# Seven raw input blocks in a state space layer, later list transposes and joined last value blocks: one decoder step on one core

## The chip, the cores and the metric

One core of a Trainium2 chip runs one launch of the kernel. The metric is the time on the device in microseconds (us). The kernel before was timed three times: 2629.93, 2630.28 and 2636.83, median 2630.28.

## The reference

One inference step of a two-layer trunk for 304 tokens: 16 meta tokens, 8 samples of 4 tokens, a prompt of 256. All numbers are float32, the width is 1024.

- Layer 0: rms norm, RWKV-7 time mixing, added to h; then rms norm and a PEER feed-forward, added to h.
- Layer 1: the same with a Mamba-2 state space layer (`in_proj` to 5152 columns, a causal convolution of width 4 with Silu on 3072 of them, decays from `softplus(dt)`, a chunked scan over 32 heads in 4 groups, a gate `silu(z)`, a group norm, `out_proj`), then PEER again and a final rms norm.

```python
def rms_norm(x, g):
    y = x * rsqrt(mean(x * x, -1) + 1e-5)
    return y * g
# state space layer
zxbcdt = xn @ in_proj
conv = conv_b + sum(full[:, j:j + L] * conv_w[j] for j in range(4))
xbc = silu(conv); dt = softplus(dt_raw + dt_bias)
# PEER: 8 heads, two lists of 128 keys per head, the 16 best sums of 16 x 16 pairs
sv, si = top_k(s, 16); cand = sv[:, :, 0, :, None] + sv[:, :, 1, None, :]
top_s, pos = top_k(cand, 16); gate = softmax(top_s)
out = sum over the 128 chosen experts e of  gate_e * gelu(x . u_e) * v_e
```

An rms norm is one divisor per token, so that `(h*g/rms) @ w` is `((h*g) @ w)/rms`: a product can be made from `h*g` and divided afterwards.

## The kernel before

Rows live with features on partitions and tokens along the free axis. Products that need float32 are made of three passes: weight and row are split in a high part (`whi`, `xh`, a cast on ACT at L279) and the rest (`wlo`, `xl`, a subtraction on DVE at L286 or on POOL at L284); `mm3` (L301) issues 24 matmuls for a block of 128 output columns, first 16 with `whi`, then 8 with `wlo`. Raw weights come by SP's DMA queue into three buffers (`wraw`); `whi` and `wlo` have two each.

**PEER (`peer`, run once per layer).** Its instructions are ordered by a planner that plays them on a timeline (L1687); what `keep_in_program_order` marks stays where the text has it. After the norm and the queries come 56 blocks `s_chunk(b)` of expert scores: 24 matmuls into `psc` (L305, L306, L308), Gelu on ACT (L1080), and `wlo` wholly on POOL. Beside them DVE runs three list searches as generators (`topk(0)` for 48 or fewer single tokens, `topk(1)` and `topk(2)` for 128 prompt tokens each), one or two steps a block. Each ends with three late pieces (L1018 to L1048): `exps` on ACT (an exponential with its table load), `gates` on DVE (sum, reciprocal, product, L1022 to L1024) and for lists 1 and 2 `finish`: three transposes on PE (`ptk`, L1029) of the row index `af`, the column index `bf` and the gate `ts`, and a copy into `sel` (L1032). The table `AFTER` at L1090 says behind which block each list's three pieces stand: list 1 at 29, 31, 39, list 2 at 46, 46, 52. After block 55 come the one-hot products (`onehots`, L1104, `pwt` at L1135), which read `sel`, and then 128 value blocks.

**The end of PEER.** The value blocks (L1248 to L1289) add 12 matmuls each into four accumulators `acc[i]` (token half `i // 2`, column half `i % 2`), in the order of the three passes; only block 127 is sorted by `i`. After it, layer 0 copies the accumulators (ACT and DVE in turn), transposes them (`pot`, L1314) and adds them to h (L1317); layer 1 adds them to rows (L1299) and norms these (`normed`, L1210).

**The state space layer (`mamba`).** It has no planner of its own; the scheduler orders each engine by readiness and by the order of the text. `prenorm` (L333) makes `xh`, `xl` from `h*g`, before the rms is known; the squares, the first product and the rms follow (`rmsnorm`, L310). `proj(blk)` makes one block of `in_proj`. The first `NU = 4` blocks (40, 32, 36, 16) use the rows that are not yet divided; their readers multiply by `ri`, the reciprocal of the rms (L1386, L1417). When the fifth begins (L1363), `xh` and `xl` are split anew from `xn = h*g*ri`, which `rmsnorm` has made (L331), with a high priority. Raw weights 40 and 32 are split at the very start, their `wlo` on POOL (L284). `decays` (L1409) makes from block 40 a long chain of small DVE instructions: the softplus as a polynomial (L1424 to L1434), two scans, and `L` and `R` (L1447 to L1452); then for each of 4 groups, 3 chunks and 2 halves a masked copy `rh` of `R` on POOL (L1489), a product `pe` on PE (L1492, L1493) and an exponential into `E` on ACT (L1494). `conv` (L1376) reads a block, convolves it on DVE (L1394) and applies Silu on ACT (L1397 three times 32 columns, L1400, L1401).

Of the kernel before, what the change touches and what calls it, by code (L numbers as in the profile page):

```python
# [23 lines left out]
F32 = mybir.dt.float32  # L24
F32R = mybir.dt.float32r
# [3 lines left out]
AF = mybir.ActivationFunctionType  # L29
ALU = mybir.AluOpType  # L30
# [4 lines left out]
T = 304  # L35
TP = 320
D = 1024
KB = 8
# [28 lines left out]
def chain(*gens):  # L67
    for g in gens:
        yield from g
# [157 lines left out]
class K:  # L227
# [102 lines left out]
        for k in range(KB) if out is not None else ():  # L330
            nc.vector.scalar_tensor_tensor(out[:, k], h[:, k], self.vec(g, k), ri, op0=ALU.mult, op1=ALU.mult)  # L331

    def prenorm(self, out, h, g, xh, xl, sq, rr, tag, mid):  # L333

        nc = self.nc
        for k in range(KB):
            x = nc.scalar.activation(xh[:, k], h[:, k], AF.Copy, scale=self.vec(g, k))
            self.tc.keep_in_program_order(x)
            nc.vector.scalar_tensor_tensor(xl[:, k], h[:, k], self.vec(g, k), xh[:, k].bitcast(F32), op0=ALU.mult, op1=ALU.subtract)
        self.rmsnorm(out, h, g, sq, None, tag, rr, mid)  # L340
        return rr[1]

# [508 lines left out]
    def peer(self, l, ng):  # L851

        nc, tc, a, C, V = self.nc, self.tc, self.a, self.C, self.nc.vector
# [233 lines left out]

        tk = chain(topk(0), topk(1), topk(2))

        AFTER = ((14, 16, 55), (29, 31, 39), (46, 46, 52))  # L1090
        for b in range(B0):
            s_chunk(b, G[:, b], leng=LP if b < LB else None, tag="so"[b % 2])
            next(tk, None)
# [142 lines left out]
        def slot():  # L1236
# [5 lines left out]
            used[r] = now[1]  # L1242
            return 4 * r

        ggen = chain(gather_u(range(ng)), gather())
        nleft = 128 - B0 - NF
        done = 0
        for b in range(128):  # L1248
            while done < nleft and (done <= (b + 1) * nleft // 118 or B0 + NF + done <= b + 1):
                t = hs[:, done % 2 * 256:done % 2 * 256 + 256]  # L1250
                s_chunk(B0 + NF + done, t, leng=LS, tag="sm"[done % 2])
                V.tensor_mul(G[:, B0 + NF + done], G[:, B0 + NF + done], t)
                done += 1
            if b == 112 and last:
                gfin = gview(24, (128, D))
                nc.sync.dma_start(gfin, a["nfin"].to_broadcast([128, D]))
            if b == (120 if last else 122):
                nc.sync.dma_start(self.h, hd)
            if b == 124 and last:

                ht = []
                for i in range(2):
                    t = gview(32 + 4 * i, (128, D))
                    for half in range(2):
                        ph = self.bank([128, 512], "ph", "s")
                        for k in range(4):
                            mm(ph[:, k * 128:k * 128 + 128], lhsT=self.h[:, 4 * half + k, 48 + 128 * i:176 + 128 * i], rhs=C["eye"],  # L1267
                               is_transpose=True, start=True, stop=True)
                        nc.scalar.copy(t[:, half * 512:half * 512 + 512], ph)
                    ht.append(t)  # L1270

                nc.scalar.activation(fin[:, 3, 3:4], C["cst"][:, 0:1], AF.Sqrt)
            raw = self.wp.tile([128, 8, 128], F32, name="wraw", tag="wraw", bufs=3) if b < RB else gview(32 + 4 * (b % RN), (128, 8, 128))
            nc.sync.dma_start(raw, a[f"v{l}"][b].rearrange("a (k d) -> a k d", d=128))
            vh = self.wp.tile([128, 8, 128], F32R, name="whi", tag="whi")
            vl = self.wp.tile([128, 8, 128], F32R, name="wlo", tag="wlo")
            self.split(vh, vl, raw, leng=LV)
            gh = tp.tile([128, 256], F32R, name="gh", tag="w1", bufs=W1)
            gl = tp.tile([128, 256], F32R, name="glo", tag="w2", bufs=W1)
            self.split(gh, gl, G[:, b])  # L1280

            vhf, vlf = (w.rearrange("p k d -> p (k d)") for w in (vh, vl))
            todo = [(i, g, w) for g, w in ((gh, vhf), (gl, vhf), (gh, vlf)) for i in range(4)]
            if b == 127:
                todo.sort(key=lambda x: x[0])
            for i, g, w in todo:
                t0, d0 = i // 2 * 128, i % 2 * 512
                mm(acc[i], lhsT=g[:, t0:t0 + 128], rhs=w[:, d0:d0 + 512], start=b == 0 and g is gh and w is vhf,  # L1288
                   stop=b == 127 and w is vlf)  # L1289
            now[0] = b  # L1290
            while b >= G0 and stepped <= (b - G0) * steps // (G1 - G0):
                next(ggen, None)
                stepped += 1
# [9 lines left out]
        for i, pt in enumerate(self.gpt):  # L1303
            hk = self.h[:, 4 * i:4 * i + 4, 0:16 * ng].rearrange("p k (g t) -> p k g t", t=16)
            V.tensor_add(hk, hk, pt.rearrange("p k (g t) -> p k g t", t=32)[:, :, 0:ng, 0:16])
        for i in range(4):
            ot = gview(100 + 2 * i, (128, 512))
            if i % 2:
                V.tensor_copy(ot, acc[i])
            else:  # L1310
                nc.scalar.copy(ot, acc[i])
            pt = self.bank([128, 4, 128], "pot", "s")
            for j in range(4):
                mm(pt[:, j], lhsT=ot[:, j * 128:(j + 1) * 128], rhs=C["eye"], is_transpose=True, start=True, stop=True)  # L1314
            t0 = 48 + i // 2 * 128
            hk = self.h[:, i % 2 * 4:i % 2 * 4 + 4, t0:t0 + 128]
            V.tensor_add(hk, hk, pt)  # L1317
# [3 lines left out]
    def mamba(self):  # L1321
# [15 lines left out]
        tok = pp.tile([128, 3, 128], F32, name="tok")  # L1337
        cdb = pp.tile([128, 10, 32], F32, name="cdb")
        mk = pp.tile([128, 3, 128], BF, name="mk")
        V.tensor_copy(mk[:, 2], C["eye"])  # L1340
        self.psum(i=2, G=2, f=2, t=2)
        ep = st.enter_context(tc.tile_pool(name="ep", bufs=4, reuse_waits="tile"))

# [2 lines left out]
        TM = T - M0  # L1346
        LM = 8
        LE = 8
        NU = 4
        done = [0]  # L1350
        pre = {b: self.load_w(a["win"][b], leng=LE, raw=raws[b]) for b in (40, 32)}
        xn = ep.tile([128, KB, T], F32, name="xn", tag="E")
        rr = ep.tile([128, 2, T], F32, name="rr", tag="E")

        def proj(blk):

            if done[0] and blk == 40:
                return first.pop()
            w = pre.pop(blk) if blk in pre else self.load_w(a["win"][blk], leng=LE if done[0] < LM else None,
                                                                    raw=raws.get(blk))  # L1360
            c0 = M0 if blk < 16 else 0
            p = self.bank([128, T - c0], "pi", "i" if done[0] % NU < 2 or done[0] >= NU else "f")
            if done[0] == NU:  # L1363
                with tc.high_priority(offset=200):
                    for k in range(KB):
                        self.split(xh[:, k], xl[:, k], xn[:, k])
            done[0] += 1
            self.mm3(p, w, (xh[:, :, c0:], xl[:, :, c0:]))
            return p

        first = []
        ri = self.prenorm(xn, self.h, "nm1", xh, xl, ep.tile([128, KB, T], F32, name="sq", tag="E"), (rr[:, 0], rr[:, 1]), "t",
                          lambda: first.append(proj(40)))
        gp = st.enter_context(tc.tile_pool(name="mg", bufs=2, reuse_waits="tile"))

        def conv(blk):  # L1376
# [16 lines left out]
            for j in range(1, 4):  # L1393
                V.scalar_tensor_tensor(ac, s[:, j:j + 328], self.vec("cw", 24 * j + blk), ac, op0=ALU.mult, op1=ALU.add)  # L1394
            r = gp.tile([128, 384], F32, name="xc", tag="xc", bufs=8)
            for c in range(3):
                nc.scalar.activation(r[:, 32 * c:32 * c + 32].rearrange("p (b t) -> p b t", t=4),  # L1397
                                     ac[:, 0:56].rearrange("p (b t) -> p b t", t=7)[:, :, 0:4], AF.Silu)

            nc.scalar.activation(r[:, 96:128], ac[:, 56:88], AF.Silu)  # L1400
            nc.scalar.activation(r[:, 128:384], ac[:, 72:328], AF.Silu)  # L1401
# [5 lines left out]
        E = []  # L1407

        def decays(dp):  # L1409
# [6 lines left out]
            x = t384("x"); xs = t384("xs")[:, 0:T]  # L1416
            V.tensor_mul(xs, p, ri)  # L1417
            tc.keep_in_program_order(V.tensor_copy(mk[:, 0:2], nm))
            p = xs
            for dst, src in ((x[:, 0:96].rearrange("p (c t) -> p c t", t=32), p[:, None, 16:48].to_broadcast([128, 3, 32])),  # L1420
                             (x[:, 96:128], p[:, 0:32]), (x[:, 128:384], p[:, 48:T])):
# [60 lines left out]
            for g in range(4):  # L1482
                Eg = ep.tile([128, 3, 8, 128], F32, name="E", tag="E")
                for ti in range(3):
                    ts = slice(ti * 128, ti * 128 + 128)
                    for q in range(2):
                        h4 = slice(8 * g + 4 * q, 8 * g + 4 * q + 4)
                        rh = dp.tile([128, 4, 128], F32, name="rh", tag="rh", bufs=2)
                        P.tensor_mul(rh, R[:, None, ts].to_broadcast([128, 4, 128]),  # L1489
                                     C["dl"][:, h4][:, :, None].to_broadcast([128, 4, 128]))  # L1490
                        pe = self.bank([128, 4, 128], "pe", "G")
                        mm(pe, lhsT=L[:, ts], rhs=rh, start=True, stop=False)  # L1492
                        mm(pe, lhsT=mk[:, 2], rhs=mk[:, min(ti, 1)][:, None, :].to_broadcast([128, 4, 128]), start=False, stop=True)  # L1493
                        nc.scalar.activation(Eg[:, ti, 4 * q:4 * q + 4], pe, AF.Exp)  # L1494
                E.append(Eg)
# [224 lines left out]
```

## Time and profile before

| | |
|---|---|
| median of the three runs | 2630.28 us |
| the profiled execution | 2634.19 us |
| its span, first to last instruction | 2632.3 us |
| mean granted TensorE clock, as a share of full speed | 0.974 |
| PE busy | 2477.9 us (94%) |
| DVE busy | 1898.8 us (72%) |
| ACT busy | 1253.6 us (48%) |
| POOL busy | 1008.2 us (38%) |

Times in the rows below are us from the first instruction. Busy means that an engine has an instruction under way; matmuls are pipelined, so that a busy PE can still run at half its clock. A wait is the idle time of an engine just before an instruction, put down to the engine and line that released it. The layers lie at: RWKV to 413, PEER of layer 0 from 413 to 1331, the state space layer to 1700, PEER of layer 1 to the end.

### The profile page before, as it was taken

Reading aid. Unit: us, or ns where it says so; the run is one execution under the profiler, and the core shown is the slowest. Engines: PE = TensorE matmul, PEld = TensorE weight load, DVE = VectorE, ACT = ScalarE, POOL = GpSimd, SP = SyncE. Lnnn points to the kernel's source line nnn. Section 1 sums busy time; section 2 is a strip of 40 time slices with the busy share of each in tenths; the row PEclk is TensorE's granted clock in tenths of the full one; section 3 lists DMA queues with packets and bytes.
Section 4 is the critical chain, followed back from the end, with each engine's and each line's share of the span. In section 5 each row is a group of like instructions: output and inputs, shape, how many; then the busy total and the mean of one; then the engine's idle time right before and its main releaser. Section 6 shows DMA issues by size and latency. Waiting matters only on the chain. (4 is left out here: it accounts for less than half of the span.)

```text
span 2632.3 us, 47459 instructions
## 1 busy us (share of the span) xinstructions
PE 2477.9 (94%) x18281; PEld 2137.4 (81%) x18281; DVE 1898.8 (72%) x3724; ACT 1253.6 (48%) x2384; POOL 1008.2 (38%) x863
## 2 busy tenths in 40 slices
PE   7999999996989999999978988999889899999998
PEld 4677768996978888888864886989789788888886
DVE  5355556797695678788784887769949756776777
ACT  3322223453784444444456543335448644444444
POOL 4111110495980233533146555117769401223210
PEclk9999999998999999999989999999989999999999
DMA  3111115453416788888732443555543267787774
GB/s 142 51 45 50 47 55 170 141 183 121 134 40 215 250 312 309 299 306 299 273 110 80 156 164 118 160 177 154 168 122 98 84 213 257 255 285 268 261 265 157
DMA packets 125858, 460.34 MB, mean 175 GB/s; under 512 B 14816, under 2 KB 15744, under 8 KB 122432
## 3 DMA queue, kind: packets, MB, share of 16 engines
q1 hardware_dynamic: 99488, 360.75, 42.1%
q0 software_dynamic: 26144, 96.56, 10.2%
q8 instruction: 144, 2.36, 0.4%
q14 instruction: 82, 0.67, 0.1%
HBM read 440.70 MB, written 16.56 MB: 174 GB/s over the span
## 5 line engine op out<-in xcount | busy, mean ns | idle before, releaser
L279 ACT CAST whi<-wraw 128x1024 fp32r<-128x1024 f32 (+1 forms) x619 | 642.1, 1038 | 870.7 <-PE acc L1288 312.9
L286 DVE TENSOR_TENSOR wlo<-wraw,whi 128x1024 fp32r<-128x1024 f32 (+1 forms) x493 | 593.7, 1204 | 397.2 <-ACT whi L279 339.6
L305 PE MATMUL psc<-xh,whi 128*128 128x256 f32 x2048 | 506.6, 285 | 3.1 <-ACT h L1080 2.6
L306 PE MATMUL psc<-xl,whi 128*128 128x256 f32 x2048 | 504.8, 283 | 0.0
L284 POOL TENSOR_TENSOR wlo<-wraw,whi 128x1024 fp32r<-128x1024 f32 (+1 forms) x150 | 355.1, 2374 | 176.5 <-ACT whi L279 91.0
L305 PEld LDWEIGHTS psc<-xh,whi 128*128 128x128 f32 x2048 | 388.0, 189 | 10.0 <-ACT h L1080 3.1
L306 PEld LDWEIGHTS psc<-xl,whi 128*128 128x128 f32 x2048 | 388.6, 190 | 5.5
L1066 POOL DMA_INDIRECT G<-in_un,gi x80 | 114.5, 1432 | 468.5 <-DVE glo L286 304.6
L1288 PE MATMUL acc<-whi,glo 128*128 128x512 f32 x1024 | 285.1, 399 | 6.7 <-DVE glo L286 6.7
L308 PE MATMUL psc<-xh,wlo 128*128 128x256 f32 x2048 | 290.3, 283 | 0.0
L1288 PE MATMUL acc<-whi,gh 128*128 128x512 f32 x1024 | 283.9, 398 | 1.9 <-ACT gh L279 1.0
L1288 PE MATMUL acc<-wlo,gh 128*128 128x512 f32 x1024 | 281.8, 397 | 0.0
L308 PEld LDWEIGHTS psc<-xh,wlo 128*128 128x128 f32 x2048 | 263.0, 188 | 0.5 <-issue 0.3
L1288 PEld LDWEIGHTS acc<-whi,glo 128*128 128x128 f32 x1024 | 193.8, 190 | 54.8 <-DVE glo L286 7.6
L1288 PEld LDWEIGHTS acc<-wlo,gh 128*128 128x128 f32 x1024 | 192.7, 189 | 47.8 <-DVE wlo L286 1.3
L1163 POOL DMA_INDIRECT G<-in_v,gi x80 | 117.0, 1463 | 298.2 <-DVE G L1158 163.8
L1288 PEld LDWEIGHTS acc<-whi,gh 128*128 128x128 f32 x1024 | 185.0, 189 | 40.3 <-ACT whi L279 1.6
L1135 PE MATMUL pwt<-ob,oa 128*128 128x128 f32 x1024 | 144.8, 282 | 11.6 <-DVE ob L1109 7.8
L1135 PEld LDWEIGHTS pwt<-ob,oa 128*128 128x128 f32 x1024 | 127.8, 191 | 23.2 <-issue 19.3
L305 PE MATMUL pi<-xh,whi 128*128 128x304 f32 (+1 forms) x328 | 102.5, 331 | 11.7 <-ACT xh L279 3.7
L286 DVE TENSOR_TENSOR glo<-G,gh 128x256 fp32r<-128x256 f32 x256 | 106.9, 419 | 2.7 <-ACT gh L279 2.7
L279 ACT CAST gh<-G 128x256 fp32r<-128x256 f32 x256 | 101.8, 399 | 11.7 <-PE acc L1288 11.6
(484 smaller groups left out, 4444.0 us busy)
## 6 DMA issues: line engine op xcount, KB each, us to landing
wraw<-in_u SPq DMA_DIRECT2D x256, 512.0 KB
wraw<-in_v SPq DMA_DIRECT2D x256, 512.0 KB
wraw<-in_win SPq DMA_DIRECT2D x41, 512.0 KB
wraw<-in_wq SPq DMA_DIRECT2D x32, 512.0 KB
wraw<-in_rkv SPq DMA_DIRECT2D x24, 512.0 KB
h<-in_ssm SPq DMA_DIRECT2D x8, 1024.0 KB
out_sssm<-h POOLq DMA_DIRECT2D x8, 1024.0 KB
wraw<-in_wo SPq DMA_DIRECT2D x8, 512.0 KB
```

Source lines behind the costliest of these rows:

```text
L279: self.nc.scalar.copy(hi, x)
L284: self.nc.gpsimd.tensor_sub(lo[:, :n], x[:, :n], hi[:, :n].bitcast(F32))
L286: self.nc.vector.tensor_sub(lo[:, n:], x[:, n:], hi[:, n:].bitcast(F32))
L305: nc.tensor.matmul(ps, lhsT=whi[:, k], rhs=xhi[:, x0 + k], start=start and k == 0, stop=False)
L306: nc.tensor.matmul(ps, lhsT=whi[:, k], rhs=xlo[:, x0 + k], start=False, stop=False)
L308: nc.tensor.matmul(ps, lhsT=wlo[:, k], rhs=xhi[:, x0 + k], start=False, stop=stop and k == kb - 1)
L1066: nc.gpsimd.indirect_dma_start(out=rows, out_offset=None, in_=a[f"un{l}"], in_offset=bass.IndirectOffsetOnAxis(ap=gi[:, 0, g, m:m + 1], ax ...
L1135: mm(pw[:, j], lhsT=oa[:, j], rhs=ob[:, j], start=True, stop=True)
L1163: nc.gpsimd.indirect_dma_start(out=rows, out_offset=None, in_=vrows, in_offset=bass.IndirectOffsetOnAxis(ap=gi[:, 1, g, m:m + 1], axis=0))
L1288: mm(acc[i], lhsT=g[:, t0:t0 + 128], rhs=w[:, d0:d0 + 512], start=b == 0 and g is gh and w is vhf, stop=b == 127 and w is vlf)
```

## The change

The list transposes move (`AFTER`), the last two value blocks are joined and sorted by accumulator, seven blocks instead of four use the undivided rows, the second split is made piece by piece behind them without a priority, the two first `wlo` go from POOL to DVE behind `xl`, the cast of the unit matrix `mk[:, 2]` moves behind the mask's, three Silu become one that reads a repeated operand, and every third `rh` is made by four ACT instructions instead of one of POOL.

```diff
-    def prenorm(self, out, h, g, xh, xl, sq, rr, tag, mid):
+    def prenorm(self, out, h, g, xh, xl, sq, rr, tag, mid, then=None):
...
             nc.vector.scalar_tensor_tensor(xl[:, k], h[:, k], self.vec(g, k), xh[:, k].bitcast(F32), op0=ALU.mult, op1=ALU.subtract)
+        if then is not None:
+            then()
         self.rmsnorm(out, h, g, sq, None, tag, rr, mid)
...
-        AFTER = ((14, 16, 55), (29, 31, 39), (46, 46, 52))
+        AFTER = ((14, 16, 55), (29, 31, 52), (45, 45, 55))
...
+        ORD = (0, 1, 2, 3) if last else (0, 2, 1, 3)
...
-            if b == 127:
-                todo.sort(key=lambda x: x[0])
+
+            if b == 126:
+                kept = todo
+                todo = []
+            elif b == 127:
+                todo = sorted(kept + todo, key=lambda x: ORD.index(x[0]))
...
-        for i in range(4):
+        for n, i in enumerate(ORD):
             ot = gview(100 + 2 * i, (128, 512))
-            if i % 2:
+            if n % 2:
...
-        V.tensor_copy(mk[:, 2], C["eye"])
...
-        NU = 4
+        NU = 7
         done = [0]
-        pre = {b: self.load_w(a["win"][b], leng=LE, raw=raws[b]) for b in (40, 32)}
-        xn = ep.tile([128, KB, T], F32, name="xn", tag="E")
+        pre = {}
+        for b in (40, 32):
+            pre[b] = tuple(self.wp.tile([128, KB, 128], F32R, name=n, tag=n) for n in ("whi", "wlo"))
+            nc.scalar.copy(pre[b][0], raws[b])
+
+        def lows():
+            for b in (40, 32):
+                tc.keep_in_program_order(V.tensor_sub(pre[b][1], raws[b], pre[b][0].bitcast(F32)))
...
-            p = self.bank([128, T - c0], "pi", "i" if done[0] % NU < 2 or done[0] >= NU else "f")
+            p = self.bank([128, T - c0], "pi", "i" if done[0] % 4 < 2 or done[0] >= NU else "f")
             if done[0] == NU:
-                with tc.high_priority(offset=200):
-                    for k in range(KB):
-                        self.split(xh[:, k], xl[:, k], xn[:, k])
+                for k in range(KB):
+                    xn = gp.tile([128, T], F32, name="xn", tag="xdt", bufs=3)
+                    V.scalar_tensor_tensor(xn, self.h[:, k], self.vec("nm1", k), ri, op0=ALU.mult, op1=ALU.mult)
+                    self.split(xh[:, k:k + 1], xl[:, k:k + 1], xn[:, None])
...
-        ri = self.prenorm(xn, self.h, "nm1", xh, xl, ep.tile([128, KB, T], F32, name="sq", tag="E"), (rr[:, 0], rr[:, 1]), "t",
-                          lambda: first.append(proj(40)))
+        ri = self.prenorm(None, self.h, "nm1", xh, xl, ep.tile([128, KB, T], F32, name="sq", tag="E"), (rr[:, 0], rr[:, 1]), "t",
+                          lambda: first.append(proj(40)), lows)
...
-            for c in range(3):
-                nc.scalar.activation(r[:, 32 * c:32 * c + 32].rearrange("p (b t) -> p b t", t=4),
-                                     ac[:, 0:56].rearrange("p (b t) -> p b t", t=7)[:, :, 0:4], AF.Silu)
+            nc.scalar.activation(r[:, 0:96].rearrange("p (c b t) -> p c b t", b=8, t=4),
+                                 ac[:, 0:56].rearrange("p (b t) -> p b t", t=7)[:, None, :, 0:4].to_broadcast([128, 3, 8, 4]), AF.Silu)
...
             tc.keep_in_program_order(V.tensor_copy(mk[:, 0:2], nm))
+            V.tensor_copy(mk[:, 2], C["eye"])
...
-                        P.tensor_mul(rh, R[:, None, ts].to_broadcast([128, 4, 128]),
-                                     C["dl"][:, h4][:, :, None].to_broadcast([128, 4, 128]))
+                        if (6 * g + 2 * ti + q) % 3 == 0:
+                            for j in range(4):
+                                nc.scalar.activation(rh[:, j], R[:, ts], AF.Copy, scale=C["dl"][:, h4.start + j:h4.start + j + 1])
+                        else:
+                            P.tensor_mul(rh, R[:, None, ts].to_broadcast([128, 4, 128]),
+                                         C["dl"][:, h4][:, :, None].to_broadcast([128, 4, 128]))
```

## Rows read from the trace of the kernel before

**Rows 1.** Who PE waited for, over the whole span: waiting line, the releaser, us in total, times, the longest.

```profile
PE ptk L1029 <- DVE G L1024: 20.5, 2, 10.2
PE ptk L1029 <- DVE G L1016: 19.3, 2, 9.8
...
PE pe L1492 <- POOL rh L1489: 7.0, 3, 2.8
...
PE pi L306 <- DVE xl L339: 3.8, 1, 3.8
PE pi L305 <- ACT xh L279: 3.7, 1, 3.7
...
PE px L1637 <- ACT xc L1400: 3.4, 1, 3.4
...
PE ptk L1029 <- DVE G L1017: 3.0, 1, 3.0
```

**Rows 2.** PE in order of time around the list transposes, layer 0, the first one-hot products of layer 0, and layer 1: start, us, engine, line, operation, tiles, shapes, count, idle time before and its releaser.

```profile
607.37 0.27 PE L1029 MATMUL ptk<-c,G 128*128 128x128 f32 x1
...
628.15 0.47 PE L1029 MATMUL ptk<-c,G 128*128 128x128 f32 x1 [10.24 <-DVE G L1024]
...
669.26 0.39 PE L1135 MATMUL pwt<-ob,oa 128*128 128x128 f32 x2
...
1897.95 0.33 PE L1029 MATMUL ptk<-c,G 128*128 128x128 f32 x1 [3.01 <-DVE G L1017]
...
1918.49 0.48 PE L1029 MATMUL ptk<-c,G 128*128 128x128 f32 x1 [10.23 <-DVE G L1024]
```

**Rows 3.** Stretches of the span: its length, then us busy (and instructions) of PE, PEld, DVE, ACT and POOL, then the granted PE clock, the DMA share and GB/s.

```profile
500.00:600.00 100.00, 100.00 (x844) 100.00 (x843) 100.00 (x405) 52.32 (x76) 88.89 (x36) 1.00 0.61 185
607.00:628.00 21.00, 1.11 (x7) 0.59 (x5) 20.96 (x42) 0.99 (x2) 2.68 (x2) 0.60 0.19 61
628.00:640.00 12.00, 11.85 (x86) 11.86 (x87) 10.62 (x11) 7.22 (x16) 7.68 (x6) 0.84 0.19 53
...
1918.50:1930.00 11.50, 11.50 (x84) 11.50 (x85) 10.42 (x10) 7.22 (x16) 7.65 (x6) 0.84 0.18 46
...
1357.00:1389.00 32.00, 22.21 (x122) 20.57 (x122) 31.85 (x55) 20.39 (x57) 17.37 (x30) 0.86 0.16 50
1389.00:1436.00 47.00, 40.24 (x122) 18.75 (x122) 16.23 (x20) 29.77 (x49) 34.67 (x32) 0.89 0.14 45
```

**Rows 4.** DVE in order of time, layer 0: three pairs of the same line and shape, the first of each pair made while POOL was at work, or L1024 the other way round (the columns of rows 2).

```profile
585.97 3.43 DVE L1007 TENSOR_TENSOR G<-G 128x1920 bf16<-128x1920 bf16 x1
...
608.31 3.96 DVE L1011 TENSOR_TENSOR G<-G,cp 128x2048 bf16<-128x2048 f32 x1
...
620.49 1.22 DVE L1007 TENSOR_TENSOR G<-G 128x1920 bf16<-128x1920 bf16 x1
...
625.60 2.29 DVE L1011 TENSOR_TENSOR G<-G,cp 128x2048 bf16<-128x2048 f32 x1
627.80 0.29 DVE L1024 TENSOR_TENSOR G<-G 128x128 f32<-128x128 f32 x1
...
655.39 0.29 DVE L1022 TENSOR_REDUCE G<-G 128x8 f32<-128x128 f32 x1 [16.74 <-ACT G L1019]
...
655.95 1.57 DVE L1024 TENSOR_TENSOR G<-G 128x128 f32<-128x128 f32 x1
```

**Rows 5.** Groups of instructions over the whole span: line, engine, operation, tiles, shapes, count, then us busy, the mean ns of one, and the idle time of the engine before them.

```profile
L286 DVE TENSOR_TENSOR wlo<-wraw,whi 128x1024 fp32r<-128x1024 f32 (+1 forms) x493 | 593.7, 1204 | 397.2 <-ACT whi L279 339.6 <-PE psc L308 35.9 <-issue 5.0
...
L284 POOL TENSOR_TENSOR wlo<-wraw,whi 128x1024 fp32r<-128x1024 f32 (+1 forms) x150 | 355.1, 2374 | 176.5 <-ACT whi L279 91.0 <-PE pq L308 34.3 <-PE psc L308 34.2
...
L1114 ACT ACTIVATE oa<-cp,sel 128x128 f32<-128x128 f32 x192 | 69.7, 396 | 5.7 <-PE pwt L1135 3.7
...
L1489 POOL TENSOR_TENSOR rh<-R,cm 128x512 f32<-128x512 f32 x24 | 28.5, 1198 | 11.1 <-PE pe L1492 8.9 <-DVE R L1452 2.1
...
L1397 ACT ACTIVATE xc<-ac 128x32 f32<-128x32 f32 x72 | 11.3, 222 | 31.6 <-DVE ac L1394 31.5
```

**Rows 6.** DVE in order of time at the start of the state space layer.

```profile
1331.56 2.01 DVE L1340 CAST mk<-c 128x128 bf16<-128x128 f32 x1
1333.49 5.75 DVE L339 SCALAR_TENSOR_TENSOR xl<-h,vecs,xh 128x304 fp32r<-128x304 f32 x8
...
1344.92 2.05 DVE L329 RECIPROCAL rr<-rr 128x304 f32<-128x304 f32 x1 [2.59 <-ACT rr L328]
1347.01 7.56 DVE L331 SCALAR_TENSOR_TENSOR xn<-h,vecs,rr 128x304 f32<-128x304 f32 x8
...
1357.11 3.17 DVE L286 TENSOR_TENSOR xl<-xn,xh 128x304 fp32r<-128x304 f32 x8
...
1387.37 0.35 DVE L1452 COPY R<-cl 32x384 f32<-32x384 f32 x1
```

**Rows 7.** POOL in order of time there.

```profile
1331.13 4.67 POOL L284 TENSOR_TENSOR wlo<-wraw,whi 128x1024 fp32r<-128x1024 f32 x2
```

**Rows 8.** DVE in order of time at the end of the kernel.

```profile
2617.34 2.84 DVE L1223 SCALAR_TENSOR_TENSOR G<-G,fin 16x512 f32<-16x512 f32 x4
2620.80 2.48 DVE L1299 TENSOR_TENSOR G<-G,acc 128x512 f32<-128x512 f32 x4 [0.63 <-PE acc L1288]
...
2626.43 2.72 DVE L1223 SCALAR_TENSOR_TENSOR G<-G,fin 128x512 f32<-128x512 f32 x4
```

## The prediction

> **What bounds the kernel now.** The page comes first: PE is busy 94% of the span at a mean granted clock of 0.974, so time can come only from what PE waits for, from stretches at a low clock, and from the end, where no matmul is left. The second view, PE's waits by releaser, shows which waits these are [rows 1]: the list transposes `ptk` hold PE for 20.5 + 19.3 + 3.0 = 42.8 us in the two layers, and nothing else that the change touches reaches more than 7.0 us (the product of the decays behind `rh`); then 3.8 and 3.7 at the start of the state space layer and 3.4 behind a Silu. Third, PE in order of time around these transposes [rows 2]: in layer 0 the first `ptk` of list 1 goes at 607.37, the last of its three only at 628.15, after a wait on DVE's L1024; in layer 1 they go between 1897.95 and 1918.49. PE's order is written out: `finish(1)` stands behind block 39, so blocks 40 to 55 can't pass it, though none of them reads `sel`. Fourth, what each engine does meanwhile [rows 3]: from 607 to 628 PE is busy 1.11 of 21 us, DVE 20.96, POOL 2.68. DVE is simply behind with the lists, and POOL, which makes the `wlo` of the blocks, stands still with PE. From 500 to 600, where blocks flow, DVE is busy the whole time too and POOL 88.89 of 100 us.
>
> **A, the list transposes.** `finish(1)` moves from 39 to 52, `finish(2)` from 52 to 55, `exps(2)` and `gates(2)` from 46 to 45. A block is 24 matmuls; 844 of them took 100 us [rows 3], so 2.84 us a block, and the 13 blocks between 39 and 52 take 36.9 us. PE then stands at the end of block 52 at 607.4 + 36.9 = 644.3, against inputs that were there at 628.1 [rows 2]: 16.2 us to spare. In layer 1 it had waited 3.0 us already at 1897.95 [rows 1, 2], so 1894.9 + 36.9 = 1931.8 against 1918.5: 13.3 to spare. If DVE's pace stayed, both waits would go whole. The granted clock also goes: after the stall it was 0.84 for 12.0 and 11.5 us [rows 3], worth 0.16 of these, 1.9 + 1.8 us. At most 42.8 + 3.7 = 46.5 us.
>
> DVE's pace won't stay. In the stall it had no POOL beside it; now blocks run on. The same instructions in both settings stand in [rows 4]: L1007 took 3.43 us among POOL's work and 1.22 in the stall, L1011 3.96 and 2.29, L1024 1.57 and 0.29. Together the first two went from 3.51 to 7.39, a factor of 2.1. The reductions among the rest show no such growth in these rows, and I take half of DVE's work as growing: 21 us × 0.5 × 1.1 = 11.6 us later in layer 0, and 23.0 (3.0 + 10.2 + 9.8, [rows 1]) × 0.5 × 1.1 = 12.7 us in layer 1, just inside 16.2 and 13.3. This "half" is the weakest number here; nothing growing and everything growing by L1007's 2.8 are its two ends.
>
> The Trainium skill bears on this (SBUF — State Buffer, "Who interferes with whom"): DVE and GpSimd share one pair of ports as an exclusive lock; a DVE instruction with two inputs in SBUF contends with a GpSimd instruction that reads SBUF, and `tensor_reduce` on trn2 never contends. Rows 4 agree for the three two-input instructions. By that rule the reductions are free and only the two-input part grows, which is the half taken; a lock held for whole POOL instructions each time would be the second rival.
>
> What hid the one-hots was their lead: DVE was ready with lists early enough that the first `pwt` came only at 669.26 [rows 2]. Now `sel` of list 1 comes at about 645 and of list 2 three blocks (8.5 us) later at 653. The first one-hots read list 1 alone and have those 8.5 us. I allow 1.5 us for what doesn't fit. `gates(2)` follows its exponential on ACT, which DVE awaited 16.74 us [rows 4]; it moves up with PE. A = −45.
>
> **B, the start of the state space layer.** POOL's two `wlo` took 4.67 us [rows 7], and beside them DVE took 2.01 us for the cast of `mk` before the first `xl` [rows 6]. The cast leaves, the two `wlo` go to DVE behind all `xl` at 1.20 each [rows 5] (POOL's were 2.37), 2.4 us. PE's wait of 3.8 for the first `xl` [rows 1] thus goes almost whole: −3. Further on, the chain is DVE's: reciprocal to 1347.0, `xn` 7.56, splits 3.17, and `R` at 1387.37 [rows 6]. DVE was busy 31.85 of 32 us from 1357, PE only 22.21, and from 1389 PE 40.24 of 47 [rows 3]: 9.8 + 6.8 us of PE's idle time lie here. Ahead of `R`, 7.56 + 3.17 = 10.7 us can leave DVE, and nine products of three more undivided blocks come in; no row prices these in this setting, so I bound them by DVE's 0.29 for a 128×128 product and 2.05 for a 128×304 reciprocal [rows 4, 6], 2.6 to 18 us, and take 0.3 each, since they are products. That leaves about 8 us for `R`, if the scheduler puts the seventh block's splits behind `decays`; in front of it, about nothing. PE meanwhile has three more blocks that wait for no split, so the wait of 3.7 for `xh` [rows 1] goes. 8 of 24 `rh` leave POOL (1.198 each, 9.6 us in all) for four ACT instructions at 0.396 (the nearest ACT row of 128×128), 1.6 us each, 12.7 in all [rows 5]; ACT was busy 29.8 of 47 us there [rows 3], so it has room for 12.7 in 17.2. Of the 7.0 us that PE waits for `rh` [rows 1] a third to a half might go; if ACT were late with its exponentials instead, the 8 × (1.6 − 1.2) and more could come back as a loss of up to 6. I take −1.5. In all 3 + 3.7 + 1.5 and some 3 of the earlier `R`: B = −11. The ends are 0, if `decays` bounds the stretch as before, and −24, if all idle time goes (9.8 + 6.8 + 3.8 + 3.7).
>
> **C, one Silu for three.** 72 of 0.222 us [rows 5] become 24. ACT isn't what PE waits for but for 3.4 us at one place [rows 1]. −1, between 0 and −3.4.
>
> **D, the joined blocks.** PE does the same 24 matmuls of 126 and 127 in another order, so that the first accumulator is complete some 9 matmuls earlier. At the end DVE was busy with earlier rows to 2620.18, waited 0.63 for the first accumulator, then added for 2.48 [rows 8]; only that 0.63 can go in layer 1, about as little in layer 0. −1. As block 127's weights are now wanted up to 9 matmuls sooner, it may also lose: ±4.
>
> **Sum.** −45 − 11 − 1 − 1 = −58. The profiled execution took 2634.2, 3.9 above the median of 2630.3: 2576.2 on its scale, 2572 on the median's.
>
> **The rivals.**
> 1. *The state space layer gains nothing*, as its chain through `decays` on DVE and the exponentials on ACT only slides. For it: DVE is full up to `R`, and the splits stay in the same stretch. Against: PE's idle time there is 24 us, and two waits have named causes that leave. 2572 + 11 = about 2583.
> 2. *POOL holds DVE more than half of the time*: all list work grows as the two pairs do, by 2.1 to 2.8, say 2.45. Layer 0: 21 × 1.45 − 16.2 = 14.3 us late; layer 1: 23 × 1.45 − 13.3 = 20.1. 34 us of A come back: 2606. For it: L1007 and L1024 grew by more than 2.1. Against: from 500 to 600 DVE already ran beside POOL, and such pairs are a part of its work.
> 3. *The waits only move along* to blocks 52 and 55, because DVE's work itself is ordered behind the blocks (one or two list steps a block). For it: DVE waited 16.74 us on ACT's exponential, which stands in that order. Against: DVE never idled in the stall. A gives nothing: 2572 + 45 = 2617.
> 4. *Slower*: POOL's `wlo` locks DVE out during all of it. Place: list work still open at 607 and 1895. With a factor f, the lateness is 21(f − 1) − 16.2 + 23(f − 1) − 13.3, and it eats A, B, C and D (about 58) from f = 3.0. At 3.5 it is 80 us: 2572 + 80 = 2652. For it: L1024's 1.57 against 0.29. Against: that instruction is tiny, and the long ones show 1.7 and 2.8.
>
> **How the numbers follow.** Forecast 0.60, rival 1 0.17, rival 2 0.13, rival 3 0.05, rival 4 0.05. The forecast's own range is 2558 to 2580: B at −24 with C and D at their best below, a few us of one-hots above. The range goes on over rival 1 to the middle of rival 2, 2555 to 2606, and leaves out rivals 3 and 4 and the half of 2. About 0.3% (8 us) is what a measurement of this kernel can tell from no change; all cases but the fourth are below that, the third at times hardly: faster 0.93, same 0.02, slower 0.05.
>
> **What would show it.** PE's waits at `ptk` under 2 us in all, blocks 40 to 52 at 2.84 us each with a clock of 1.00, and L1007 and L1011 of list 1's end at their slow durations; a wait at `ptk` of 10 to 20 us would be rival 2, one of 20 us and an idle DVE rival 3. The first `pi` matmul on `xl` about 3 us after the layer's start, seven blocks without a wait for `xh`, `R` earlier by 1 to 10 us, and fewer waits of `pe`. A `pwt` that waits for one-hots by more than a few us would be an error of A; PE waiting for `whi` or weights of block 127, one of D. Wrong as a whole it would be if DVE's list work took over 30 us longer than before.

## The result, and the profile after

The changed kernel takes 2593.8 us (median of four, 2589.8 to 2599.2) against 2631.5 before, a ratio of 0.9855 with a 95% interval of 0.9831 to 0.9878: 37.7 us faster, where 58 were forecast, inside the range of 2555 to 2606. One of the four executions of e4, below, took 3434.26 us at a granted clock of 0.648 and isn't counted.

PE's waits of the changed kernel, over the whole span, answer to [rows 1] (same columns):

```profile
PE pg L1572 <- DVE G L1569: 11.7, 3, 8.6
...
PE ptk L1031 <- DVE G L1026: 6.6, 2, 4.7
PE pe L1510 <- ACT rh L1505: 5.5, 2, 5.1
PE pi L305 <- ACT xh L279: 5.4, 1, 5.4
PE pi L305 <- DVE cst L1400: 4.7, 1, 4.7
...
PE px L1655 <- ACT xt L1656: 2.1, 1, 2.1
...
PE pwt L1137 <- DVE ob L1120: 1.5, 1, 1.5
PE pe L1510 <- POOL rh L1507: 1.5, 2, 1.3
```

The 42.8 us at `ptk` are 6.6 now. The first `xl` is no wait any more. In the state space layer 5.4 us for `xh`, 4.7 for `cst`, 5.1 for the first `rh` and 8.6 for `G` stand there now, where the longest waits for these tiles were 3.7, 2.6, 2.8 and 2.9.

To see where the time went, both traces are cut at the same events: from the first score matmul to the last `pwt` in each PEER, and from the last `pot` to layer 1's second norm (the state space layer). The columns are those of [rows 3]. Before:

```profile
485.57:783.81 298.24, 271.12 (x2221) 263.89 (x2220) 258.46 (x839) 186.26 (x412) 238.18 (x170) 0.97 0.40 122
1772.96:2074.09 301.13, 271.28 (x2221) 263.90 (x2220) 261.31 (x839) 185.79 (x413) 238.87 (x170) 0.96 0.39 120
1330.89:1721.11 390.22, 340.80 (x2006) 286.24 (x2006) 296.46 (x396) 192.71 (x435) 188.48 (x224) 0.93 0.40 133
```

And after:

```profile
480.68:763.43 282.75, 271.62 (x2221) 263.94 (x2220) 275.22 (x839) 186.10 (x412) 245.88 (x170) 0.99 0.42 128
1748.42:2032.45 284.03, 271.09 (x2221) 263.71 (x2220) 278.15 (x839) 185.80 (x413) 246.46 (x170) 0.99 0.42 128
1310.29:1695.92 385.63, 334.70 (x2007) 280.23 (x2006) 293.48 (x407) 201.67 (x414) 173.19 (x214) 0.92 0.40 134
```

The two PEERs give 15.5 and 17.1 us, the state space layer 4.6. That is 37.2 of the 41.9 us between the two spans (2632.3 and 2590.4). Another 4.9 lie ahead of layer 0's PEER (480.68 against 485.57), in code that is the same, and stand for how far one execution differs from another: in e11, the changed kernel once more, this PEER begins at 483.54. The rest of the span gives −0.2. The state space layer's gain lies wholly ahead of the first `pg` (a product of the scan) that waits, 1.7 us for POOL's `cst`; this one comes 180.3 us after the layer's start instead of 184.9; from there to the layer's end it is 205.3 us in both, the new wait of 8.6 for `G` included. PE does the same work, but DVE's 839 instructions of the first stretch take 275.2 us instead of 258.5.

At the end of the kernel nothing moved. DVE in order of time there, to be laid beside [rows 8]:

```profile
2575.41 2.84 DVE L1225 SCALAR_TENSOR_TENSOR G<-G,fin 16x512 f32<-16x512 f32 x4
2578.87 2.48 DVE L1306 TENSOR_TENSOR G<-G,acc 128x512 f32<-128x512 f32 x4 [0.63 <-PE acc L1295]
```

### The profile page after: what moved, and what is told of

Read it like the earlier page. It is cut to its first block, busy times and chain, and to the rows that moved or that the text cites. A ratio compares the mean times of both kernels' runs of the same rounds, so it can differ in the third digit from the quotient of the medians.

```text
span 2590.4 us, 47437 instructions
## 1 busy us (share of the span) xinstructions
PE 2468.9 (95%) x18281; PEld 2129.3 (82%) x18281; DVE 1930.5 (75%) x3735; ACT 1262.8 (49%) x2363; POOL 1009.2 (39%) x853
## 3 DMA queue, kind: packets, MB, share of 16 engines
q1 hardware_dynamic: 99488, 360.75, 42.8%
## 5 line engine op out<-in xcount | busy, mean ns | idle before, releaser
L284 POOL TENSOR_TENSOR wlo<-wraw,whi 128x1024 fp32r<-128x1024 f32 (+1 forms) x148 | 363.4, 2465 | 152.4 <-ACT whi L279 95.2
L305 PE MATMUL pi<-xh,whi 128*128 128x304 f32 (+1 forms) x328 | 97.2, 316 | 11.0 <-ACT xh L279 5.4
```

Of the source, the lines that this page charges most:

```text
L284: self.nc.gpsimd.tensor_sub(lo[:, :n], x[:, :n], hi[:, :n].bitcast(F32))
L305: nc.tensor.matmul(ps, lhsT=whi[:, k], rhs=xhi[:, x0 + k], start=start and k == 0, stop=False)
```

## The experiments

Stage times are read from each run's trace by the same cuts; one execution each. The median is that of the counted executions. e1 to e12 are edits of the kernel before or of the changed one; e11 is the changed one itself.

| run | median us | PEER, layer 0 | PEER, layer 1 | state space layer |
|---|---|---|---|---|
| before | 2631.5 | 298.2 | 301.1 | 390.2 |
| changed | 2593.8 | 282.8 | 284.0 | 385.6 |
| e1 lists only | 2602.2 | 283.7 | 284.3 | 392.2 |
| e2 lists back | 2630.8 | 298.7 | 302.9 | 386.1 |
| e3 exponential earlier | 2589.6 | 279.1 | 284.3 | 386.2 |
| e4 low parts left out | 2584.6 | 277.1 | 278.7 | 385.0 |
| e5 split early | 2588.7 | 279.2 | 285.2 | 385.0 |
| e6 all `rh` on POOL | 2602.2 | 284.9 | 287.2 | 391.6 |
| e7 four raw blocks | 2596.0 | 283.4 | 284.4 | 385.7 |
| e8 e5 and e6 | 2594.8 | 283.6 | 284.1 | 388.6 |
| e9 lists and `rh` | 2597.1 | 283.8 | 284.5 | 386.6 |
| e10 e3 and e5 | 2591.2 | 279.3 | 285.6 | 385.8 |
| e11 changed again | 2592.9 | 279.2 | 284.1 | 386.4 |
| e12 half of `rh` on ACT | 2597.7 | 279.2 | 284.2 | 389.3 |

The table has its own measure of chance: where the code of a stage is that of the changed kernel, layer 0's PEER took 279.2 to 284.9 us, but the state space layer only 385.0 to 386.4 (five runs). With the old state space layer it took 390.2 and 392.2 (before and e1). In layer 0's PEER the two groups differ in a wait: where `ptk` waited 1.3 to 1.9 us (changed, e1, e6 to e9) it took 282.8 to 284.9, where it didn't (e5, e11, e12) 279.2.

**Which half of the change gave the gain.** e1 is the kernel before with

```diff
-        AFTER = ((14, 16, 55), (29, 31, 39), (46, 46, 52))
+        AFTER = ((14, 16, 55), (29, 31, 52), (45, 45, 55))
```

and e2 the changed kernel with the first of these lines. Expected of e1:

> The kernel before with the table AFTER of the changed kernel and nothing else of the change. Theory: the moved transposes bring nearly all of the gain, some 16 us in each layer (PE from the first score block to the last pwt: 298.2 us before, 282.7 in the changed kernel; 301.1 and 284.0 in layer 1), so 2631 - 33 = 2598. Rival: the rest of the change carries half of the gain; then this one stands at 2612 or more.

Expected of e2:

> The changed kernel with the old table AFTER, so that all but the list transposes is changed. Theory: the state space layer brings 4 to 5 us and the joined blocks and the Silu under 1 us, so 2631 - 5 = 2626, with the old waits of about 43 us at ptk. Rival: half of the gain sits here, 2612.

e1 came to 2602.2, 0.9885 [0.9861, 0.9909] of the kernel before, e2 to 2630.8, 0.9987 [0.9973, 1.0002]. The lists carry some 30 us in the time and 31 in the stages; the rest has 4 to 6 us in its own stage, which the time of e2 alone can't tell from none. The rivals fall.

**What ate part of the lists' gain.** In the changed kernel the same list work takes DVE nearly twice as long as in the stall. DVE in order of time, layer 0, from list 2's L995 to the gate product of list 1 (L1026), which is what `ptk` waits for:

```profile
605.39 0.98 DVE L995 MAX8 G<-G 128x8 f32<-128x50 f32 x8
606.30 4.02 DVE L1013 TENSOR_TENSOR G<-G,cp 128x2048 bf16<-128x2048 f32 x1
...
612.64 3.42 DVE L1017 TENSOR_TENSOR G<-G 128x2048 bf16<-128x2048 bf16 x1
615.98 2.43 DVE L999 CAST G<-G 128x128 f32<-128x128 uint32 x1
618.33 2.27 DVE L1018 TENSOR_REDUCE G<-G 128x128 f32<-128x2048 bf16 x1
...
625.81 3.42 DVE L1009 TENSOR_TENSOR G<-G 128x1920 bf16<-128x1920 bf16 x1
...
634.11 2.29 DVE L1019 TENSOR_TENSOR G<-G 128x128 f32<-128x128 f32 x1
...
640.93 2.44 DVE L1026 TENSOR_TENSOR G<-G 128x128 f32<-128x128 f32 x1
```

That is 38.0 us (605.39 to 643.37). Run e4 keeps the order and takes POOL away: the third pass of blocks 38 to 52 reads `whi` in place of `wlo`, so the low part of these weights is left out.

```diff
-            w = self.load_w(a[f"u{l}"][b], heng=heng, leng=leng)
+            if 38 <= b <= 52:
+                raw = self.fetch(a[f"u{l}"][b])
+                hi = self.wp.tile([128, 8, 128], F32R, name="whi", tag="whi")
+                nc.scalar.copy(hi, raw)
+                w = (hi, hi)
+            else:
+                w = self.load_w(a[f"u{l}"][b], heng=heng, leng=leng)
```

> The changed kernel, but blocks 38 to 52 of the scores take their high weights a second time in place of the low ones (the low part is left out there), so that PE has the same matmuls and POOL has nothing beside the last list work. Theory: POOL is what stretches DVE's list work, 37.9 us from L995 of list 2 to the gates of list 1 in the changed kernel against 20.6 in the stall of the kernel before; here it comes back to 20 to 23 us, no wait at ptk is left, and the gain is 7 to 10 us against the changed kernel. Rival: it is the running PE, ACT and DMA that slow DVE; the stretch stays near 38 us and the waits stay.

The same view of e4:

```profile
602.12 0.98 DVE L995 MAX8 G<-G 128x8 f32<-128x50 f32 x8
603.02 2.27 DVE L1013 TENSOR_TENSOR G<-G,cp 128x2048 bf16<-128x2048 f32 x1
...
606.85 1.21 DVE L1017 TENSOR_TENSOR G<-G 128x2048 bf16<-128x2048 bf16 x1
607.99 0.21 DVE L999 CAST G<-G 128x128 f32<-128x128 uint32 x1
608.12 2.27 DVE L1018 TENSOR_REDUCE G<-G 128x128 f32<-128x2048 bf16 x1
...
613.51 1.22 DVE L1009 TENSOR_TENSOR G<-G 128x1920 bf16<-128x1920 bf16 x1
...
618.09 0.28 DVE L1019 TENSOR_TENSOR G<-G 128x128 f32<-128x128 f32 x1
...
620.83 0.28 DVE L1026 TENSOR_TENSOR G<-G 128x128 f32<-128x128 f32 x1
```

19.0 us (602.12 to 621.11), with PE, ACT and the loads running on, as the stretch in the changed kernel and in e4 shows (the columns of [rows 3]):

```profile
605.39:643.37 37.98, 35.36 (x292) 34.50 (x290) 37.95 (x43) 19.57 (x29) 35.07 (x13) 1.00 0.56 168
602.12:621.11 18.99, 18.99 (x162) 18.99 (x162) 18.96 (x43) 9.07 (x14) 0.00 (x0) 1.00 0.61 194
```

No wait at `ptk` is left, the PEERs take 277.1 and 278.7, and the time is 0.9822 [0.9796, 0.9848] of the kernel before. So it is POOL that stretches the list work, and the rival falls. Line by line the growth isn't a factor: L1017 and L1009 grew by 2.2 us, L999 by 2.2, L1019 by 2.0, L1026 by 2.2, the first L1013 by 1.8, whether they last 0.2 or 2.3 us alone, and the reduction L1018 by nothing. Each that grew started while POOL had a `wlo` under way and ended only after it: L999 runs from 615.98 to 618.41, a `wlo` from 614.93 to 618.33. The `wlo` grew as well: four of them in a row took 11.35 us, 2.84 each, against 2.37 [rows 5]. In these rows who starts second waits: L1004 started 0.11 us ahead of a `wlo` and lost nothing (2.14 us in e4), and that `wlo` took 4.30. POOL's rows, and L1004 of DVE:

```profile
614.93 3.40 POOL L284 TENSOR_TENSOR wlo<-wraw,whi 128x1024 fp32r<-128x1024 f32 x1
620.64 4.30 POOL L284 TENSOR_TENSOR wlo<-wraw,whi 128x1024 fp32r<-128x1024 f32 x1
624.90 11.35 POOL L284 TENSOR_TENSOR wlo<-wraw,whi 128x1024 fp32r<-128x1024 f32 x4
...
620.53 2.17 DVE L1004 TENSOR_TENSOR G<-G,cp 128x1920 bf16<-128x1920 f32 x1
```

Run e3 looked for a cheap way out: `exps(1)` and `gates(1)` behind block 26, which puts the gate product in front of L1013 on DVE.

```diff
-        AFTER = ((14, 16, 55), (29, 31, 52), (45, 45, 55))
+        AFTER = ((14, 16, 55), (26, 26, 52), (45, 45, 55))
```

> The changed kernel with exps(1) and gates(1) behind block 26 instead of 29 and 31; on DVE the three small gate instructions of list 1 then stand in front of the big ones of list 2. Theory: what is left of the waits at ptk (1.9 and 4.7 us) is there because the gate product of list 1 stands behind L1013 of list 2 and so comes some 9 us late; with the new place both waits go, and the clock's dip behind them (0.87 for 13 us, 1.7 us a layer): about -8 us against the changed kernel. Rival: the one-hots are late all the same and PE waits for them by as much; no more than -3 us.

The product came at 631.2 instead of 640.9 and no wait at `ptk` is left, but PE's waits show what is late next:

```profile
PE pwt L1137 <- DVE ob L1111: 8.0, 32, 1.3
...
PE pwt L1137 <- DVE ob L1120: 4.9, 1, 4.9
```

The one-hots stand on DVE behind list 2, so in layer 1 the wait of 4.7 at `ptk` became one of 4.9 at the first `pwt`, and the stage takes 284.3 us against 284.0 in the changed kernel. 2589.6 against 2593.8 can't be told from chance, nor can layer 0's 279.1, since e11 has 279.2 with the changed kernel itself. The rival holds, the 8 us of the theory don't come.

**The state space layer.** Three rows each: the first 30 us, the next 30 and the next 45 (columns as above; the whole layer stands with the result). Before:

```profile
1330.89:1360.89 30.00, 21.42 (x115) 20.32 (x115) 26.73 (x45) 17.21 (x35) 13.91 (x14) 0.80 0.38 116
1360.89:1390.89 30.00, 20.25 (x114) 17.91 (x114) 29.85 (x50) 16.53 (x49) 18.57 (x31) 0.90 0.16 53
1390.89:1435.89 45.00, 38.30 (x120) 17.87 (x118) 14.34 (x15) 29.77 (x49) 33.46 (x30) 0.90 0.14 47
```

After:

```profile
1310.29:1340.29 30.00, 26.87 (x173) 24.48 (x172) 26.76 (x49) 21.52 (x40) 21.76 (x24) 1.00 0.45 142
1340.29:1370.29 30.00, 12.08 (x26) 5.82 (x26) 25.72 (x54) 16.75 (x32) 9.61 (x21) 0.60 0.14 44
1370.29:1415.29 45.00, 41.17 (x171) 25.52 (x172) 14.53 (x18) 38.99 (x79) 23.65 (x20) 0.96 0.14 38
```

Seven raw blocks run through: 173 matmuls instead of 115 in the first 30 us, at a clock of 1.00 instead of 0.80. Then PE has little: 26 instead of 114. The eighth block's split stands behind the decays. `R` did come earlier, 44.1 us after the layer's start (its last copy ends at 1354.39) instead of 56.8 (1387.72 [rows 6] less 1330.89). DVE's last copy of `R`, then PE in order of time in the hole:

```profile
1354.04 0.35 DVE L1466 COPY R<-cl 32x384 f32<-32x384 f32 x1
...
1344.84 0.61 PE L305 MATMUL pi<-xh,whi 128*128 128x288 f32 x1 [5.37 <-ACT xh L279]
1350.19 0.58 PE L305 MATMUL pi<-xh,whi 128*128 128x288 f32 x1 [4.74 <-DVE cst L1400]
1355.86 1.19 PE L1510 MATMUL pe<-rh,L 128*128 128x512 f32 x1 [5.10 <-ACT rh L1505]
```

Four runs took this apart. Run e5 gives the split its old priority:

```diff
             if done[0] == NU:
-                for k in range(KB):
...
-                    self.split(xh[:, k:k + 1], xl[:, k:k + 1], xn[:, None])
+                with tc.high_priority(offset=200):
+                    for k in range(KB):
...
+                        self.split(xh[:, k:k + 1], xl[:, k:k + 1], xn[:, None])
```

> The changed kernel, with the eight pieces of the second split (product, cast, subtraction) given the high priority that the old split had, so that they stand among the steps of the decays and not behind R. In the changed kernel PE waits 5.4 us for xh, 4.7 for cst and 5.1 for the first rh between 1339 and 1356, after seven blocks without a gap. Theory: these 15 us are the price of the late split; with it early PE runs block 8 and 9 there, R comes some 5 us later, and the state space layer, 385.6 us in the changed kernel, gets 4 to 8 us shorter. Rival: R and the exponentials behind it set the end of this stretch whatever PE does beside them; then the later R costs what the early split gives, and the layer stays within 2 us or gets up to 5 us longer.

Run e6 gives all `rh` back to POOL:

```diff
-                        if (6 * g + 2 * ti + q) % 3 == 0:
-                            for j in range(4):
-                                nc.scalar.activation(rh[:, j], R[:, ts], AF.Copy, scale=C["dl"][:, h4.start + j:h4.start + j + 1])
-                        else:
...
+                        P.tensor_mul(rh, R[:, None, ts].to_broadcast([128, 4, 128]),
+                                     C["dl"][:, h4][:, :, None].to_broadcast([128, 4, 128]))
```

> The changed kernel with all 24 rh on POOL, as before. Theory: ACT is what makes the 24 products pe last 58.3 us (47.1 before); without 12.8 us of copies and with the first rh not behind them, they take some 50 us and the layer gets 2 to 6 us shorter than 385.6. Rival: POOL was the limit, as PE's waits for rh of 7.0 us in the kernel before say; the waits for POOL come back and the layer gets 2 to 5 us longer.

Run e7 is `NU = 4` in place of 7:

> The changed kernel with four blocks on undivided rows instead of seven; all else stays, the late split too. Theory: the seven blocks are worth what PE does while DVE makes the decays; with four PE runs dry three blocks (some 12 us) earlier, waits for the split by 10 to 15 us more, and gets back part of it later: the layer 5 to 12 us longer than 385.6. Rival: PE isn't what limits this stretch, the decays are; the layer stays within 2 us.

Run e8 is e5 and e6 together:

> Both edits of the two runs before: the second split early and all rh on POOL. If both theories hold their gains add up to 6 to 14 us; if R sets the stretch, nothing beyond the better of the two.

The layer took 385.0, 391.6, 385.7 and 388.6 us. The theory of e5 and that of e7 both fall and their rivals hold: in the changed kernel an earlier split and the number of raw blocks are each worth under 1 us. The early split and the `rh` aren't independent, though: with all `rh` on POOL the early split is worth 3.0 us (e8 against e6). e7's rows show why the three blocks don't count:

```profile
1316.96:1346.96 30.00, 18.17 (x105) 16.57 (x104) 26.71 (x53) 20.01 (x41) 18.61 (x22) 0.81 0.40 133
1346.96:1376.96 30.00, 23.06 (x99) 16.09 (x100) 23.17 (x49) 19.02 (x48) 11.28 (x22) 0.73 0.06 19
1376.96:1421.96 45.00, 39.41 (x163) 23.37 (x162) 11.97 (x10) 37.72 (x71) 23.08 (x22) 0.96 0.22 67
```

105 and 99 matmuls instead of 173 and 26: after 105 us it has 367, the changed kernel 370. The same work is done in another order. Matmuls that are ahead are no proof of a gain either: e5 has 396 by then, and its layer is 0.6 us shorter than the changed kernel's. e6 moved the layer most, by 6.0 us, against its theory: the products `pe` do take 50 us instead of 58, from 45.4 to 95.0 after the layer's start, yet the layer is back where the kernel before was, although `R` comes as early as in the changed kernel. Its rival had the direction: `pe` waits 8.2 us for `rh` and 2.9 for `E` there, against 7.0 and 0.4 in the changed kernel. In the third stretch it has 147 matmuls where the changed kernel has 171, although PE is busy as long (40.68 and 41.17 us); the granted clock is 0.87 against 0.96:

```profile
1377.08:1422.08 45.00, 40.68 (x147) 21.41 (x148) 13.77 (x14) 25.51 (x44) 25.83 (x26) 0.87 0.20 70
```

A new theory, then: the layer's gain is that of the `rh` on ACT and nothing else. Run e9 tests it from the other side, as the kernel before with the new `AFTER` and that one edit:

> The kernel before with two edits alone: the changed table AFTER, and every third rh on ACT. Theory: the rh are all that the state space layer's rewrite brought; the seven blocks, the late split, the low parts on DVE and the single Silu cancel out. Then the layer takes 385 to 387 us here (392.2 with the lists alone, 385.6 in the changed kernel) and the whole is that of the changed kernel within 3 us, 2591 to 2597. Rival: rh on ACT help only together with an early R and more blocks at hand; then the layer stays at 390 to 392 and the time at 2600 to 2604.

386.6 us for the layer, against 392.2 in e1 and 385.6 in the changed kernel, with four raw blocks and `R` as late as before (57.9 us after the start, 1374.97 less 1317.06). The whole layer in e1, e9 and e6:

```profile
1315.34:1707.56 392.22, 342.35 (x2006) 288.07 (x2006) 298.64 (x396) 192.78 (x435) 188.86 (x224) 0.92 0.40 132
1317.06:1703.62 386.56, 338.44 (x2006) 281.88 (x2007) 294.70 (x396) 203.79 (x469) 180.55 (x216) 0.93 0.40 134
1317.08:1708.69 391.61, 339.51 (x2005) 280.78 (x2006) 301.66 (x407) 185.00 (x376) 178.78 (x222) 0.91 0.39 132
```

The theory holds within 1.6 us, since the changed layer takes 385.0 to 386.4. How much the `rh` are worth depends on what stands beside them: 6.0 us in the changed kernel, 5.6 here, 3.6 where the split is early (e8 against e5). The time is 2597.1, 0.9861 [0.9844, 0.9879], beside 0.9854 [0.9839, 0.9869] for the changed kernel once more (e11): on the edge of what was expected, and no difference that can be told.

Run e12 asks whether more of it helps, with `% 2 == 1` for `% 3 == 0`, which also puts the first `rh` on POOL:

> The changed kernel with every second rh on ACT instead of every third (12 of 24), and the first one on POOL. Theory: a third is near the balance; ACT is busy 39 of 45 us from 60 to 105 us after the layer's start, and four more rh are 6.4 us more, so the layer gets no shorter than 386 and at worst 4 us longer. Rival: POOL's share still limits the stretch and each rh on ACT is worth 6.0/8 = 0.75 us; then the layer takes 382 to 383 us.

389.3 us: a third is better than half, and the rival falls. ACT's busy time in the third stretch hardly rose, from 38.99 to 39.28 us, while fewer matmuls went through:

```profile
1371.72:1416.72 45.00, 38.44 (x158) 24.24 (x159) 12.33 (x17) 39.28 (x86) 18.86 (x16) 0.91 0.11 35
```

**Together.** Run e10 joins e3 and e5; e11 is the changed kernel once more.

> The changed kernel with exps(1) and gates(1) behind block 26 and the second split with the early priority, the two edits that came out below it. If they add up, 4 + 1 to 5 us under the changed kernel: 2585 to 2590. If the difference of the single runs was chance, 2592 to 2595.

> The changed kernel once more, beside the two, for their comparison: 2594, between 2590 and 2599.

2591.2 and 2592.9, with overlapping intervals (0.9824 to 0.9851 and 0.9839 to 0.9869). The lower medians of e3 and e5 don't add up, and no run that does all the work beats the changed kernel by more than its uncertainty. e4, which leaves work out, comes nearest: its other three executions (2582.6 to 2586.1) lie under all eight of the changed kernel (2589.8 to 2599.2), but the intervals touch.

## Why the prediction was right, and where it was not

- **Bound and place.** Right: the time was in the waits at `ptk`, and blocks 40 to 52 run past them. Of 42.8 us of waits 6.6 are left, where under 2 was the sign.
- **The total.** 2593.8 is not in the forecast's own range of 2558 to 2580; it lies between rivals 1 and 2, inside a range that had been drawn over both. That range's lower end was added up wrong as well: −45 − 24 − 3.4 − 4 is −76, which is 2554 and not 2558.
- **A, forecast −45, measured −32.6** (15.5 + 17.1; −36.0 in e11). The step that failed is the "half of DVE's work as growing", 11.6 us in layer 0 and 12.7 in layer 1. Measured from L995 to the gate product the work takes 38.0 against 20.7 us (607.41 to 628.09) in the stall of layer 0, 17.3 more, and 38.2 against 19.0 in layer 1, 19.2 more. Two things shift the slack of 16.2 and 13.3. Counted from the first score block, L995 starts 2.9 and 1.4 us later than before, which takes from it; and the 13 blocks take 38.6 and 39.2 us instead of 36.9, which adds 1.7 and 2.3 to it but is a loss of its own. Together that makes waits of 2.3 and 5.0; they were 1.9 and 4.7. In e11 L995 of layer 0 isn't late, and `ptk` doesn't wait there. Most of what is missing of the 45 is thus 6.6 of waits and 4.0 of slower blocks. The first `pwt` waited 1.5, the allowance made for it, by luck: it waits 0 to 3.1 us in layer 0 of other runs of this code. With POOL quiet (e4) the two stages are 21.1 and 22.4 us shorter, 43.5, near the forecast's 45: the slack arithmetic was sound, and POOL's share of what is missing is 10.9 us against the changed kernel's profile, 7.5 against e11's.
- **Its form was wrong too.** I multiplied durations by 2.1. The growth is what is left of the `wlo` that an instruction meets, 0.8 to 2.2 us for those that grew, whatever their own length, and nothing for the reductions; so their number is what counts. The rule of the Trainium skill (SBUF — State Buffer, "Who interferes with whom") of an exclusive lock held for a whole instruction describes this better than my factor, and its word on `tensor_reduce` agrees (L1018: 2.27 us in both). Rival 2, which had the lock, was too heavy by its price: 34 us for 7.5 to 10.9.
- **B, forecast −11, measured −4.6** (−6.6 against e1, which has the old layer too). The front went as said: the cast takes 0.22 us, the eight `xl` 3.65 instead of 5.75, the wait for them is gone. `R` came 12.7 us earlier, more than the 8 I took. But none of this shows in the layer: e9 has neither and is as fast within 1.6 us. The "some 3 of the earlier `R`" and the 3.7 at `xh` were nothing: the hole from 1340 has waits of 5.4, 4.7 and 5.1. "PE meanwhile has three more blocks" was true and no gain, since they only come sooner (e7). The smallest term, the `rh` at −1.5, is all that the runs leave of B, 3.6 to 6.0 us (e6, e8, e9). Its reason was wrong: a third to a half of the 7.0 us that PE waits for `rh` was to go, and these waits are 5.5 + 1.5 = 7.0 now. So B's sign was right for another reason than the ones given. Rival 1 was right about the blocks and blind to this.
- **C and D.** The wait of 3.4 behind the Silu is gone, another of 2.1 stands at the same product; no run takes C alone, and no gain shows in the layer once e9 is taken off. D is nothing: DVE still waits 0.63 for the first accumulator, so that term was wrong by its small size.
- **Rivals 3 and 4.** DVE never waited for blocks in the old stall's place, and its factor of 1.8 is far from 3.0.

## What to carry to other kernels

When a stall goes, the engine that was late loses the quiet in which it caught up: price its work with the neighbours running, by instructions that meet them and not by time. Blocks that are ready sooner help only if the stretch behind them has work left; compare at a common later point before booking the gain, and as late a one as the trace has (e5). A small shift between two engines that feed the same product can be worth more than the large rewrite around it, so try it alone.

## What was not expected of the hardware

A one-input cast of 128x128 (L999) grows as much beside POOL as the two-input instructions, 0.21 to 2.43 us. POOL's own `wlo` pay for it as well, 2.84 us against 2.37. In the hole of the state space layer PE's granted clock is 0.60 in the mean of 30 us, near the lower of its two levels (1.2 of 2.4 GHz), where it had been at 1.00 in the 30 us before. That the layer pays for this isn't shown: e5 and e7 fill part of the hole, and the layer moves by under 1 us.

What stays open is how the eight `rh` on ACT bring this. PE's waits for `rh` hardly changed in sum (5.7 on POOL in e1, 5.2 on ACT and 2.1 on POOL in e9). The rows of e1, e9 and e6, with that of the changed kernel, say where the time is: the same 2006 matmuls keep PE busy 3.9 us less in e9 than in e1, and 4.8 less in the changed kernel than in e6, while its idle time falls by only 1.8 and 1.2. So most of it is matmuls that go through in less time, not waits. The granted clock is higher by 0.01 both times; whether that or closer packing of the products of the blocks among the `pe` does it, no run isolates.
